# Two first projection tiles ordered by hand, the last tile's q and k and the group matrices moved, two attention groups combined on another engine

## The chip, the cores and the metric

The kernel runs on one core of a Trainium2 chip. The core has a matrix engine (TensorE, PE in the profile), a vector engine (VectorE, DVE), a scalar engine (ScalarE, ACT), a general engine (GpSimd, POOL) and SyncE (SP), which here only issues transfers. Each engine works through its own instructions in order and waits for others by semaphores. SP, ACT and POOL each have a DMA queue. The metric is the device time of one launch in microseconds (us), less is better.

## What is computed

One layer of a diffusion backbone for 256 prompt tokens and 2048 latent tokens of width 1024. Cut to what matters:

```python
h = rms_norm(x, norm1_g) * (1 + sc1) + sh1
q, k, v, f = project(h, w_in, q_norm_g, k_norm_g)      # q, k normalised by head half; 512 columns each
q, k = rope(q), rope(k)                                # latent tokens only
s = einsum('bqhmd,bkhmd->bhmqk', q, k) * scale         # 4 heads, 2 halves m
p = softmax(s)
attn = (p[:, :, 0] - lam * p[:, :, 1]) @ v             # latent tokens: 512 cached and 2048 own keys
four = fft2(f, axes=(positions, channels)).real @ w_four[group]
x = x + g1 * concat(rms_norm(attn, subln_g), four) @ w_out
x = x + g2 * relu(h2 @ w1) ** 2 @ w2
```

`lam` comes from four lambda vectors, `sc`, `sh` and `g` from conditioning vectors.

## The kernel before

Products are done at single precision in three passes, high by high, low by high and high by low parts (`mm3`, L86 to L88), so each operand is split into a rounded half and a rest: a cast on ACT, a subtraction on DVE. The stages follow one another: conditioning and head (to 41 us), first projection with the weights' splitting (to 66), the other projection tiles (to 501), Fourier mixing (to 595), attention (to 1355), output projection, MLP.

**Projection.** There are 18 tiles of 128 tokens, 0 and 1 of the prompt, 2 to 17 latent. `proj(i, g)` multiplies tile i by one of four column groups (0 q, 1 k, 2 v, 3 Fourier) into a PSUM bank, `PJ`, of which there are four, 24 products each. Ahead of it stand `norm` (L178 to L186: square on ACT, power on POOL, scale on DVE), `transposed` (transposes on PE, L195; copies with the modulation on ACT, `hTa`, L198; `hh` and `hl`, L229 and L230). Behind it `squares` (L245 to L250), `qk_post` (L259 to L293: `qn`, the rope or gain table `tb`, `qo`, `qt`), `v_post` (copy `vo`, L345, stores and split) and `f_post` (`fo`, L364). Tile 0 is special: the weights `w_in` come in halves and are split in the same loop over eight k steps (`wh` on ACT, L480, `wl` on DVE, L481), and the tile's own modulated transpose is made by `h_mod` (L457, L459), one column block on ACT and the next on DVE in turn, all into one tile `hTa0`. `setup_gains` (L109) fetches q and k gains and the four lambda vectors (`lq`) by six transfers of ACT's queue and works them out. A loop for tiles 1 to 16 follows; its order is left to the framework's scheduler, as is the head's.

**Written order.** From the last tile (17) on, the code stands in `tc.manual_schedule()`: each compute engine takes its instructions as written. There the Fourier operands start: f is folded with its reversed rows (`ds` and `rv` loads by SP; `e2048(t)` on DVE makes the difference `e`, split into `E_h` and `E_l`, and the sum in `rv`, whose row 0 is replaced by `mid`, L596); `O` are the split sums. Cosine matrices (`c2048`, `com`/`co`) and sine matrices (`s2048`, `som`/`so`), 512 KB for each of four row blocks, in the order 3, 2, 1, 0, come on POOL's queue (`dft`, L553). `E` against `c2048` gives `pabE` (48 products), `O` against `s2048` gives `pabo`. The group matrices `pabw` (L758, L759: eight small products of `wf` = w_four with `c128`, `s128`) are split into `cwh` and `cwl` (L763 to L766) and multiply every result (`py`). `evac` (L642 to L646) takes a bank out as high and low part (`abhE`, `ablE`). `head_T2` transposes the last tile's q and k (`qkT17`), which go to DRAM (`kd`, `qd`) for attention. `etmp` are two loads of the prompt's f.

**Attention.** For each of four heads, eight groups of 256 queries; a group has four units (two query blocks j, two halves m). A unit is five score blocks of 512 keys (`fill`, L875, into five PSUM banks), five row maxima on DVE (L880), five exponentials on ACT (L899). After both halves of a j, `combine` (L901 to L921) forms P0 - factor * P1 on POOL in four operations, scaled in place (L920) and added (L921), and in the very last group on DVE by five operations (L911). Then come transposes of P (`pts`, L930), their parts (`ahs` on ACT, `als` on DVE) and value products (`mul`). The order is by due times: a unit every T = 5.2, the transposes of a group from AVS = 6 units after its first.

Of the kernel before, what the change touches and what calls it, by code (L numbers as in the profile page):

```python
# [18 lines left out]
P = 128  # L19
D = 1024  # L20
KD = D // P
# [19 lines left out]
def body(tc, a, out):  # L41
    nc = tc.nc
    ctx = ExitStack()
    with ctx:
# [64 lines left out]
        def setup_gains(pool):  # L109
            for t, n, s in ((qg, "q_norm_g", 0.125), (kg, "k_norm_g", 1.0)):  # L110
                nc.scalar.dma_start(t[:, 0:64], a[n].partition_broadcast(P).rearrange("p o d -> p (o d)"))
# [5 lines left out]
            lq = pool.tile([P, 4, 64], F32, tag="t2", name="lq", bufs=6)  # L117
            for i, n in enumerate(("lambda_q1", "lambda_q2", "lambda_k1", "lambda_k2")):
                nc.scalar.dma_start(lq[:, i, :], a[n].partition_broadcast(P).rearrange("p o d -> p (o d)"))
# [84 lines left out]
        with ExitStack() as c1:  # L204
# [54 lines left out]
            def qk_post(i, ms=(0, 1), dst=None):  # L259
                s = i < 2  # L260
                if ms[0] == 0:
                    rope_load(i)
# [77 lines left out]
            def v_post(i):  # L340
                s = 1 if i < 2 else 0
                n = i if s else i - 2
                ps = PJ.pop((i, 2))
                o = t2(f"vo{i}")
                nc.scalar.copy(o, ps)  # L345
                nc.sync.dma_start(out[3][n * P:n * P + P] if s else vs[n * P:n * P + P], o)
                v_split(s, n if s else 4 + n, o, f"v{i}")
# [51 lines left out]
            with tc.manual_schedule():  # L399
# [30 lines left out]
                with tc.tile_pool(name="p0h", bufs=6, reuse_waits="tile") as halves:  # L430
# [10 lines left out]
                    for s in range(2):  # L441
                        for j in range(4):
                            nc.tensor.matmul(pm[:, 12 + j, s:s + 1], acc[s][:, j * P:(j + 1) * P], ones, start=True, stop=True)
                    for gi in range(3):
                        r = t2(f"mr{gi}")
                        (nc.vector.tensor_copy if gi == 1 else nc.scalar.copy)(r[0:2, :], pr[gi][0:2, :])
                        for j in range(4):
                            nc.tensor.transpose(pm[:, gi * 4 + j, :], r[0:2, j * P:(j + 1) * P], ident[0:2, 0:2])
                    nc.vector.tensor_add(modc[:, 0:16, :], pm, cols[:, 32:48].unsqueeze(2).to_broadcast([P, 16, 2]))
                    mk_scale(scale1, 8, 80)  # L450
                    hT = p1.tile([P, KD, P], F32, tag="hT", name="hTa0", bufs=1)
                    HH.update({i: tuple(p1.tile([P, KD, P], F32R, tag=f"h{x}", name=f"h{x}{i}") for x in "hl") for i in range(2)})

                    def h_mod(pt, k, eng):
                        sc, sh = scale1[:, k, 1:2], modc[:, k, 1:2]
                        if eng is nc.vector:
                            nc.vector.tensor_scalar(hT[:, k, :], pt[:, k % 4, :], sc, sh, op0=ALU.mult, op1=ALU.add)  # L457
                        else:
                            nc.scalar.activation(hT[:, k, :], pt[:, k % 4, :], AF.Identity, bias=sh, scale=sc)  # L459

                    def h_low(i, c):
# [1176 lines left out]
```

## Time and profile before

| | |
|---|---|
| three runs | 3042.86, 3044.54 (median), 3053.85 us |
| profiled execution: time, span | 3056.93 us, 3054.9 us |
| mean granted TensorE clock | 0.985 |
| busy: PE, DVE, ACT, POOL | 2948.1, 2019.7, 1574.5, 1054.5 us |

The profile is that of one execution. An engine's busy time is the sum of its instructions, the rest of the span it is idle. A timeline lists instructions with the idle time ahead of each and what released it; a view by stretches gives busy times and the granted clock of a part of the span. A product of 128x512 starts 0.23 us after the one before at full clock.

### The profile page before, as it was taken

The numbers are of one execution on the slowest core, as the hardware profiler recorded it, in microseconds if no ns is written. First come the engines' busy times: TensorE is split into PE (matmuls) and PEld (weight loads), VectorE is DVE, ScalarE is ACT, GpSimd is POOL, SyncE is SP. The second block draws the span as 40 slices with busy tenths as digits, with TensorE's granted clock in tenths as the row PEclk, the third lists the DMA queues.
The fourth block names the chain that finished last, engine by engine and source line by source line (L and its number), as shares of the span: only waits on it lengthen the run. The fifth ranks groups of instructions, "written<-read, shape, count | busy, mean of one in ns | idle before, by whom it ended". The sixth has DMA issues, their size and how long they took to land.

```text
span 3054.9 us, 43872 instructions
## 1 busy us (share of the span) xinstructions
PE 2948.1 (97%) x15417; PEld 2546.2 (83%) x15417; DVE 2019.7 (66%) x3370; ACT 1574.5 (52%) x3534; POOL 1054.5 (35%) x843
## 2 busy tenths in 40 slices
PE   7999998989999999989989999999999999999998
PEld 4888886768888888878879999999998887888887
DVE  6566775578888888874457667667665355454554
ACT  4233322578888888863345555555555322232221
POOL 0111112088898899852233334334332000000000
PEclk8999999999999999999999999999999999999999
DMA  7677878422121201126755546456456377555553
GB/s 275 166 198 190 222 195 261 165 76 82 34 108 42 104 31 57 69 70 205 226 167 168 168 162 213 163 166 212 163 168 224 134 248 247 172 204 168 197 206 104
DMA packets 398670, 490.87 MB, mean 161 GB/s; under 512 B 27555, under 2 KB 308208, under 8 KB 395378
## 3 DMA queue, kind: packets, MB, share of 16 engines
q1 hardware_dynamic: 390352, 473.44, 48.0%
q10 hardware_dynamic: 5506, 8.07, 0.8%
q0 software_dynamic: 2592, 6.55, 0.6%
q8 instruction: 122, 2.00, 0.3%
q14 instruction: 98, 0.80, 0.1%
HBM read 318.87 MB, written 171.18 MB: 160 GB/s over the span
## 4 chain that ended last, share of the span: by engine, by line
PE 81%; ACT 8%; DMA 4%; DVE 4%; issue 2%; POOL 1%; SPq 0%; ACTq 0%; POOLq 0%; DVEq 0%
PE ps L88 7%; PE ps L86 7%; PE ps L87 7%; PE Ss L875 7%; PE pj L86 4%; PE pj L87 4%; PE pj L88 4%; PE pts L930 3%; ACT P1s L899 3%; PE pC L1351 2%; PE pC L1350 2%; PE pC L1352 2%; PE pA L1350 2%; PE pA L1352 2%; PE pA L1351 2%; PE po L88 2%
## 5 line engine op out<-in xcount | busy, mean ns | idle before, releaser
L880 DVE TENSOR_REDUCE mxs<-Ss 128x1 f32<-128x512 f32 x640 | 419.5, 687 | 91.5 <-PE Ss L875 82.7
L921 POOL TENSOR_TENSOR P0s<-P0s,P1s 128x1024 f32<-128x1024 f32 x126 | 372.8, 2959 | 10.5
L1283 DVE TENSOR_TENSOR sl<-sr,sh 128x768 fp32r<-128x768 f32 x168 | 161.7, 964 | 279.0 <-ACT sh L1282 275.2
L1282 ACT CAST sh<-sr 128x768 fp32r<-128x768 f32 x168 | 139.7, 834 | 342.0 <-PE ps L87 335.7
L899 ACT ACTIVATE P1s<-Ss,mxs 128x512 f32<-128x512 f32 x320 | 217.1, 693 | 65.7 <-DVE mxs L883 65.7
L86 PE MATMUL pj<-wh,hh 128*128 128x512 f32 x576 | 232.4, 404 | 7.0 <-ACT vo L345 7.0
L86 PE MATMUL ps<-thT,sh 128*128 128x512 f32 x585 | 231.0, 395 | 4.8 <-ACT sh L1282 4.8
L88 PE MATMUL ps<-thT,sl 128*128 128x512 f32 x585 | 230.8, 395 | 0.5 <-DVE sl L1283 0.5
L87 PE MATMUL pj<-wl,hh 128*128 128x512 f32 x576 | 230.8, 401 | 0.2 <-DVE wl L481 0.2
L87 PE MATMUL ps<-tlT,sh 128*128 128x512 f32 x585 | 230.7, 394 | 0.0
L88 PE MATMUL pj<-wh,hl 128*128 128x512 f32 x576 | 229.0, 398 | 0.0
L1392 POOL TENSOR_TENSOR gs<-g,g 128x384 f32<-128x384 f32 x48 | 68.8, 1433 | 448.6 <-ACT g L1362 404.9
L899 ACT ACTIVATE P0s<-Ss,mxs 128x512 f32<-128x512 f32 x320 | 215.6, 696 | 10.1 <-DVE mxs L883 7.9
L875 PE MATMUL Ss<-KS1s,Qs 128*128 128x512 f32 x640 | 200.4, 427 | 13.9 <-ACT P0s L899 12.2
L1361 ACT ACTIVATE g<-uz 128x384 f32<-128x384 f32 x144 | 75.7, 526 | 251.0 <-DVE uz L1384 226.9
L875 PE MATMUL Ss<-KS0s,Qs 128*128 128x512 f32 x640 | 195.9, 418 | 8.2 <-ACT P1s L899 4.9
L930 PEld LDWEIGHTS pts<-ident,P0s 128*128 128x128 f32 x1280 | 158.8, 142 | 52.2 <-PE Ss L875 5.7
L930 PE MATMUL pts<-ident,P0s 128*128 128x128 f32 x1280 | 193.1, 274 | 6.3 <-DVE alp L1027 4.1
L920 POOL TENSOR_SCALAR P1s<-P1s,tots 128x1024 f32<-128x1024 f32 x126 | 169.1, 1342 | 5.7
L86 PE MATMUL ps<-ophT,sh 128*128 128x512 f32 x423 | 166.7, 394 | 2.6 <-ACT sh L1282 1.5
L941 DVE TENSOR_TENSOR als<-pts,ahs 128x512 fp32r<-128x512 f32 x256 | 163.9, 682 | 5.5 <-ACT ahs L936 5.4
L88 PE MATMUL ps<-ophT,sl 128*128 128x512 f32 x423 | 166.6, 394 | 0.8 <-DVE sl L1283 0.8
(575 smaller groups left out, 8277.1 us busy)
## 6 DMA issues: line engine op xcount, KB each, us to landing
sr<-sd SPq DMA_DIRECT2D x84, 768.0 KB, 4.8
a<-in_w SPq DMA_DIRECT2D x184, 256.0 KB, 3.5
b<-in_w SPq DMA_DIRECT2D x176, 256.0 KB, 4.6
sd<-gs SPq DMA_DIRECT2D x192, 192.0 KB, 1.8
sd<-g SPq DMA_DIRECT2D x144, 192.0 KB, 1.9
wm<-in_w_mod SPq DMA_DIRECT2D x32, 512.0 KB, 5.3
Qs<-qd SPq DMA_DIRECT2D x32, 512.0 KB, 3.4
hr<-hd SPq DMA_DIRECT2D x21, 768.0 KB, 5.5
```

Source lines behind the costliest of these rows:

```text
L86: nc.tensor.matmul(ps, lh, rh, start=first, stop=False)
L87: nc.tensor.matmul(ps, lh, rl, start=False, stop=False)
L88: nc.tensor.matmul(ps, ll, rh, start=False, stop=last)
L875: nc.tensor.matmul(S[:, :w], self.Q[:, x, m, j * P:j * P + P], self.hd.KS[m][:, b * 512:b * 512 + w], start=(x == 0), stop=(x == 1))
L880: nc.vector.tensor_reduce(self.mx[j][:, m, b:b + 1], self.S[j, m, b], axis=AX.X, op=ALU.max)
L899: nc.scalar.activation(dst, S, AF.Exp, bias=self.mx[j][:, m, 6:7], accum_out=self.sm[j][:, m, b:b + 1])
L920: nc.gpsimd.tensor_scalar(p, p, tot[:, 3:4], 0.0, op0=ALU.mult, op1=ALU.add)
L921: nc.gpsimd.tensor_add(d, d, p)
L930: nc.tensor.transpose(pt[:, c:c + P], self.p0[j][:, (kb + t) * P:(kb + t + 1) * P], ident)
L941: nc.vector.tensor_sub(t, self.pt[kb], f32(self.A[kb][0]))
L1282: nc.scalar.copy(hi, src)
L1283: nc.vector.tensor_sub(lo, src, f32(hi))
```

## The change

Four places change; the products are the same in number and operands.

- First tiles: `h_mod` does tile 0's first four blocks on ACT and the others on DVE, into two tiles; one of the modulation rows goes ahead of the conditioning products; `load_gains` is split off from `setup_gains`, on POOL's queue and earlier. Tile 2's load, tile 1's split and tile 2's norm stand inside the weight loop. Tile 0's `f_post` and `v_out` (a part of `v_post`), then tile 1's first two projections and tile 0's remaining work are written in order inside the manual schedule, tile 3's load behind them. The loop over tiles skips those for i = 1.
- Last tile: its rope table is loaded first; `c128`, `s128` and `wf` come on POOL's queue right after the cosine matrices; `qk_post` for q and k alternates with `e2048(1)` and `e2048(0)`; the row copy from `mid` is on POOL; the O splits are moved behind the E products; in the built program the loads of `etmp` stand ahead of those of rv1 and rv0 on SP's queue.
- Group matrices: `group_mats(0)` ahead of the E products, `group_mats(1)` behind; the evacuations of E are spread; `head_T2` takes q at step 0 and k at step 2.
- Attention: in the first two groups of head 0 the j = 1 combination is done on DVE in five operations, and the transposes start 5 units after the first unit instead of 6.

```diff
@@ -106,17 +106,21 @@
-def setup_gains(pool):
-    for t, n, s in ((qg, "q_norm_g", 0.125), (kg, "k_norm_g", 1.0)):
-        nc.scalar.dma_start(t[:, 0:64], a[n].partition_broadcast(P).rearrange("p o d -> p (o d)"))
+def load_gains(pool):
+    for t, n in ((qg, "q_norm_g"), (kg, "k_norm_g")):
+        nc.gpsimd.dma_start(t[:, 0:64], a[n].partition_broadcast(P).rearrange("p o d -> p (o d)"))
+    lq = pool.tile([P, 512], F32, tag="ff", name="lq", bufs=4)[:, 0:256].rearrange("p (n d) -> p n d", d=64)
+    for i, n in enumerate(("lambda_q1", "lambda_q2", "lambda_k1", "lambda_k2")):
+        nc.gpsimd.dma_start(lq[:, i, :], a[n].partition_broadcast(P).rearrange("p o d -> p (o d)"))
+    return lq
...
+def setup_gains(pool, lq):
+    for t, s in ((qg, 0.125), (kg, 1.0)):
...
-    lq = pool.tile([P, 4, 64], F32, tag="t2", name="lq", bufs=6)
-    for i, n in enumerate(("lambda_q1", "lambda_q2", "lambda_k1", "lambda_k2")):
-        nc.scalar.dma_start(lq[:, i, :], a[n].partition_broadcast(P).rearrange("p o d -> p (o d)"))
@@ -258,7 +262,7 @@
-if ms[0] == 0:
+if i not in RP:
@@ -337,13 +341,19 @@
-def v_post(i):
+def v_out(i):
...
+    return o
...
+def v_post(i):
+    s = 1 if i < 2 else 0
+    n = i if s else i - 2
+    o = v_out(i)
@@ -438,42 +448,47 @@
-for s in range(2):
-    for j in range(4):
-        nc.tensor.matmul(pm[:, 12 + j, s:s + 1], acc[s][:, j * P:(j + 1) * P], ones, start=True, stop=True)
-for gi in range(3):
...
+def mod_cols(gi):
...
+mod_cols(0)
+for s in range(2):
+    for j in range(4):
+        nc.tensor.matmul(pm[:, 12 + j, s:s + 1], acc[s][:, j * P:(j + 1) * P], ones, start=True, stop=True)
+mod_cols(2)
+mod_cols(1)
...
-hT = p1.tile([P, KD, P], F32, tag="hT", name="hTa0", bufs=1)
+lq = load_gains(p1)
...
-def h_mod(pt, k, eng):
+def h_mod(dst, pt, k, eng):
...
-        nc.vector.tensor_scalar(hT[:, k, :], pt[:, k % 4, :], sc, sh, op0=ALU.mult, op1=ALU.add)
+        nc.vector.tensor_scalar(dst, pt[:, k % 4, :], sc, sh, op0=ALU.mult, op1=ALU.add)
...
-        nc.scalar.activation(hT[:, k, :], pt[:, k % 4, :], AF.Identity, bias=sh, scale=sc)
...
-def h_low(i, c):
-    nc.vector.tensor_sub(HH[i][1][:, c, :], hT[:, c, :], f32(HH[i][0][:, c, :]))
...
+        nc.scalar.activation(dst, pt[:, k % 4, :], AF.Identity, bias=sh, scale=sc)
...
+h0 = [t2(f"hTa0_{b}").rearrange("p (k t) -> p k t", k=4) for b in range(2)]
+for k in range(4):
+    h_mod(h0[0][:, k, :], pt0[0], k, nc.scalar)
+    h_mod(h0[1][:, k, :], pt0[1], 4 + k, nc.vector)
...
-    for k in range(b * 4, b * 4 + 4):
-        h_mod(pt0[b], k, nc.vector if k % 2 else nc.scalar)
-    c = slice(b * 4, b * 4 + 4)
-    nc.vector.tensor_copy(HH[0][0][:, c, :], hT[:, c, :])
-    h_low(0, c)
+    hi, lo = (x[:, b * 4:b * 4 + 4, :] for x in HH[0])
+    nc.vector.tensor_copy(hi, h0[b])
+    nc.vector.tensor_sub(lo, h0[b], f32(hi))
...
-PJ.update({(0, g): pp.tile([P, 512], F32, tag="pj", name=f"pj0_{g}", bufs=4) for g in range(4)})
+PJ.update({(0, g): pp.tile([P, 512], F32, tag="pj", name=f"pj0_{g}", bufs=4) for g in (3, 2, 0, 1)})
...
+load(2)
@@ -481,21 +496,27 @@
-            if 2 <= k < 6:
-                for x in (2 * k - 4, 2 * k - 3):
-                    h_mod(pt1[x // 4], x, nc.scalar)
+            if 1 <= k < 5:
+                for x in (2 * k - 2, 2 * k - 1):
+                    h_mod(hT[:, x, :], pt1[x // 4], x, nc.scalar)
+            if k == 5:
+                nc.scalar.copy(HH[1][0], hT)
+                nc.vector.tensor_sub(HH[1][1], hT, f32(HH[1][0]))
+            if k == 6:
+                norm(p1, X[2], "a2")
...
-        nc.scalar.copy(HH[1][0], hT)
-        h_low(1, slice(0, KD))
-        load(2)
-        setup_gains(p1)
-po = c1.enter_context(tc.tile_pool(name="p1o", bufs=2, reuse_waits="tile"))
-squares(0, 0)
-squares(0, 1)
-qk_post(0)
-v_post(0)
-f_post(0)
+    po = c1.enter_context(tc.tile_pool(name="p1o", bufs=2, reuse_waits="tile"))
+    f_post(0)
+    vo0 = v_out(0)
+    proj(1, 0)
+    squares(0, 0)
+    squares(0, 1)
+    proj(1, 1)
+    setup_gains(p1, lq)
+    qk_post(0)
+    v_split(1, 0, vo0, "v0")
+    load(3)
@@ -505,14 +526,15 @@
-if i + 1 < N1:
+if i > 1:
...
-proj(i, 0)
+    proj(i, 0)
...
-if i + 2 < N1:
+if 1 < i < N1 - 2:
...
-proj(i, 1)
+if i > 1:
+    proj(i, 1)
@@ -529,6 +551,7 @@
+rope_load(LAST)
@@ -562,6 +585,8 @@
+c128, s128 = (fa.tile([P, P], F32, tag=x, name=x, bufs=1) for x in ("c128", "s128"))
+wf = fa.tile([P, 4, P], F32, tag="wf", name="wf", bufs=1)
@@ -577,6 +602,9 @@
+nc.gpsimd.dma_start(c128, a["c128"])
+nc.gpsimd.dma_start(s128, a["s128"])
+nc.gpsimd.dma_start(wf, a["w_four"][0].rearrange("g p c -> p g c"))
@@ -593,7 +621,7 @@
-V.tensor_copy(r[0:1, :], mid[0:1, :])
+nc.gpsimd.tensor_copy(r[0:1, :], mid[0:1, :])
@@ -603,15 +631,12 @@
-for t in (1, 0):
-    e2048(t)
+for m in range(2):
+    qk_post(LAST, (m,), qko)
+    e2048(1 - m)
...
-for t in ROWS:
-    O[t] = split(DR[t][1], f"O{t}_")
-qk_post(LAST, (0,), qko)
-qk_post(LAST, (1,), qko)
@@ -723,16 +748,10 @@
-ptq = [pp.tile([P, 512], F32, tag="y", name=f"pt{LAST}_{m}", bufs=3) for m in (1, 0)]
+ptq = [pp.tile([P, 512], F32, tag="y", name=f"pt{LAST}_{m}", bufs=3) for m in range(2)]
...
-c128 = fw.tile([P, P], F32, tag="c128", name="c128")
-s128 = fw.tile([P, P], F32, tag="s128", name="s128")
-wf = fw.tile([P, 4, P], F32, tag="wf", name="wf")
-nc.sync.dma_start(c128, a["c128"])
-nc.sync.dma_start(s128, a["s128"])
-nc.sync.dma_start(wf, a["w_four"][0].rearrange("g p c -> p g c"))
@@ -747,33 +766,50 @@
-paE = [pab(f"E{g}") for g in range(4)]
-for t in (3, 2, 1, 0):
-    for g in range(4):
-        ab_mm(paE[g], g, E[t], co[t], 512, t == 3, t == 0)
-A = [evac(paE[0], 0, 512, "E0")]
-for h in range(2):
-    pw = pab(f"w{h}")
+pws, paE = [pab("w0")], [pab(f"E{g}") for g in range(4)]
+pws.append(pab("w1"))
...
+def group_mats(h):
...
-        nc.tensor.matmul(pw[:, j * 256:j * 256 + P], c128, wf[:, 2 * h + j, :], start=True, stop=True)
-        nc.tensor.matmul(pw[:, j * 256 + P:j * 256 + 256], s128, wf[:, 2 * h + j, :], start=True, stop=True)
+        nc.tensor.matmul(pws[h][:, j * 256:j * 256 + P], c128, wf[:, 2 * h + j, :], start=True, stop=True)
+        nc.tensor.matmul(pws[h][:, j * 256 + P:j * 256 + 256], s128, wf[:, 2 * h + j, :], start=True, stop=True)
...
+def group_parts(h):
...
-    pv = pw.rearrange("p (g t c) -> p g t c", g=2, t=2)
+    pv = pws[h].rearrange("p (g t c) -> p g t c", g=2, t=2)
...
-    cw += [(r[:, j], l[:, j]) for j in range(2)]
-A += [evac(paE[g], 0, 512, f"E{g}") for g in range(1, 4)]
+    cw.extend((r[:, j], l[:, j]) for j in range(2))
...
+A = [None] * 4
...
+def e_evac(g):
+    A[g] = evac(paE[g], 0, 512, f"E{g}")
...
+group_mats(0)
+for t in (3, 2, 1, 0):
+    for g in range(4):
+        ab_mm(paE[g], g, E[t], co[t], 512, t == 3, t == 0)
+group_parts(0)
+for t in range(4):
+    O[t] = split(DR[t][1], f"O{t}_")
+group_mats(1)
+e_evac(0)
+group_parts(1)
+e_evac(1)
...
+    if g < 2:
+        e_evac(g + 2)
...
-    if g < 2:
-        parts[g] = head_T2(1 - g, ptq[g])
+    if g in (0, 2):
+        parts[1 - g // 2] = head_T2(g // 2, ptq[g // 2])
@@ -849,6 +885,8 @@
+self.vcomb = 5 if self.last else 5 if hd.h == 0 and g < 2 else 0
@@ -904,14 +942,15 @@
-if self.last and j:
-    for b in range(self.hd.nbk):
+if j and self.vcomb:
+    for b in range(self.vcomb):
...
-    return
-for x in range(2):
+    if self.vcomb == self.hd.nbk:
+        return
+for x in range(j and self.vcomb // 2, 2):
@@ -1084,8 +1123,9 @@
+avs = AVS - (h == 0 and g < 2)
...
-    w = base + (AVS + q) * T
+    w = base + (avs + q) * T
@@ -1098,7 +1138,7 @@
-w = base + (AVS + 5) * T + 1.0 * u
+w = base + (avs + 5) * T + 1.0 * u
```

## The prediction

> **What bounds the kernel now.** I read the busy times first, then the same by stretches of the span, to see where TensorE (PE), which carries the kernel, is not full.
>
> ```profile
> PE 2948.1 (97%) x15417; PEld 2546.2 (83%) x15417; DVE 2019.7 (66%) x3370; ACT 1574.5 (52%) x3534; POOL 1054.5 (35%) x843
> ```
>
> ```profile
> 45.00:72.00 27.00, 22.61 (x97) 17.78 (x95) 20.87 (x40) 20.19 (x42) 1.09 (x2) 0.94 0.81 286
> 72.00:80.00 8.00, 4.74 (x11) 3.77 (x12) 6.46 (x13) 4.21 (x10) 3.46 (x2) 0.50 0.32 105
> 80.00:120.00 40.00, 40.00 (x193) 32.91 (x193) 20.99 (x36) 10.28 (x21) 6.19 (x3) 0.99 0.60 165
> 520.00:560.00 40.00, 35.38 (x161) 28.73 (x162) 24.64 (x47) 14.83 (x28) 3.17 (x6) 0.86 0.52 141
> 612.00:650.00 38.00, 28.84 (x123) 20.46 (x122) 26.34 (x51) 26.60 (x74) 28.62 (x20) 0.85 0.16 57
> 770.00:860.00 90.00, 88.92 (x556) 75.29 (x555) 78.39 (x155) 79.58 (x228) 80.64 (x64) 1.00 0.17 60
> ```
>
> Columns: stretch, length, then busy time of PE, weight loads, DVE, ACT, POOL, then granted clock, DMA share, GB/s. Within stages (80:120, 770:860) PE has no gap. The change touches three seams where it has: the first tile's end (72:80: 4.74 of 8 us, clock 0.50), the passage into the Fourier stage (520:560, 4.6 us idle) and attention's start (612:650, 9.2 us idle at clock 0.85). It neither adds nor removes a matrix product, so time can come only from gaps and from half-clock stretches.
>
> **Part 1, the first two tiles.** These rows are the timeline around the first gap.
>
> ```profile
> 36.28 0.41 DVE L457 TENSOR_SCALAR hTa<-pta,scale,modc 128x128 f32<-128x128 f32 x1 [0.53 <-ACT hTa L459]
> 65.88 0.39 PE L87 MATMUL pj<-wl,hh 128*128 128x512 f32 x1
> 66.11 0.40 PE L88 MATMUL pj<-wh,hl 128*128 128x512 f32 x1
> 70.06 0.29 DVE L120 TENSOR_TENSOR lq<-lq 128x128 f32<-128x128 f32 x1 [2.95 <-DMA lq<-in_lambda_k]
> 70.81 2.88 ACT L198 ACTIVATE hTa<-pta,modc,scale 128x128 f32<-128x128 f32 x8
> 74.53 1.23 DVE L230 TENSOR_TENSOR hl<-hTa,hh 128x1024 fp32r<-128x1024 f32 x1
> 75.06 0.65 ACT L364 ACTIVATE fo<-pj 128x512 f32<-128x512 f32 x1
> 75.26 0.80 PE L86 MATMUL pj<-wh,hh 128*128 128x512 f32 x1 [7.00 <-ACT vo L345]
> 75.85 0.63 PE L87 MATMUL pj<-wl,hh 128*128 128x512 f32 x1
> 76.28 0.63 PE L88 MATMUL pj<-wh,hl 128*128 128x512 f32 x1
> ```
>
> Columns here and in the later timelines: start, duration, engine and line, operation and tiles, and in brackets the idle time before and its releaser.
> (a) The gap. Tile 0's products end at 66.5 and tile 1's begin at 75.26, because the same ACT and DVE queues first do tile 2's transposed copies (hTa, 2.88), the lambda row (DVE waits 2.95 us for a load) and only then empty the four product banks (fo, 75.06). Afterwards the order is written out: tile 2's eight transposes (1.1 us of PE that stays) stand inside tile 0's last k step, the gains and lambda rows are loaded early from POOL's queue, and fo is the first copy. fo stands behind hTa on ACT: transposes from 63.6, hTa to 67.7, fo to 68.3. PE's last product moves to 67.2 + 0.4 = 67.6, so it still waits some 0.7. Tile 1 starts at 68.3 where it was 75.26: **-7.0**. Bounds: -7.7 if fo never waits, -5 if hTa and fo are late by 2 us.
> (b) The half clock. After the gap products start 0.43 apart (75.85, 76.28), against 0.23 ahead of it (65.88, 66.11). The 80:120 stretch with its clock of 0.99 puts the end at about 80.8, so 13 products lose 0.2 each: **-2.6** if a wait of 0.7 doesn't lower the clock, 0 if it does.
> (c) The head. The first tile's scaling alternates ACT and DVE, each waiting 0.53 for the other (row 36.28), four times over. Split by halves, four operations of 0.41 run on each side at once, and the first product comes about **-1.5** sooner (0 if the weight loads then decide).
> (d) The price: tile 1's hl (1.23, by tile 2's row of that shape) and its hh, tile 2's square and scale move into the weight loop, which feeds PE from ACT and DVE. In 45:72 DVE is idle 6.1 us and ACT 6.8, so about 2 us on each is covered on the average, but not everywhere: bounds 0 and +2, I take **+0.6**. Six DMA issues leave ACT's queue there, and take POOL's, which is busy 1.09 us in that stretch.
> Part 1: -7.0 - 2.6 - 1.5 + 0.6 = **-10.5**, bounds -3 and -12, of which -8 to -12 is my own range.
>
> On the clock, the Trainium skill (TensorE: Matmul & The Clock Gate, What's actually happening) has an idle window of some 3.4 us, running free, behind each halving. The 7.00 us gap with the 0.43 spacing behind it agrees; by that rule 0.7 us costs nothing, the same as (b) takes.
>
> **Part 2, into the Fourier stage.** First the chain of waits (start, length, what), then timelines of PE, SP's queue, POOL and DVE, and the median landing time of the second matrix's loads.
>
> ```profile
> 499.53 17.16 DMA qd<-qkT_0l
> 516.72 3.80 DMA rp<-in_rope
> ...
> 528.75 0.43 PE pabo L86
> ```
>
> ```profile
> 514.16 0.39 PE L88 MATMUL pabE<-c,E_l 128*128 128x512 f32 x1
> 521.76 0.77 PE L758 MATMUL pabw<-wf,c 128*128 128x128 f32 x2 [7.21 <-DMA wf<-in_w_four]
> ...
> 526.67 0.80 PE L758 MATMUL pabw<-wf,c 128*128 128x128 f32 x2 [2.86 <-DVE ablE L646]
> ```
>
> ```profile
> 518.00 0.38 SPq L735 DMA_DIRECT2D wf<-in_w_four  x1
> ```
>
> ```profile
> 494.24 2.37 POOL L553 DMA_DIRECT2D c<-in_c  x4
> ...
> 499.50 2.17 POOL L553 DMA_DIRECT2D s<-in_s  x4
> ```
>
> ```profile
> 506.01 0.69 DVE L593 TENSOR_TENSOR e<-ds,rv 128x512 f32<-128x512 f32 x1 [8.22 <-DMA rv<-frev]
> ...
> 510.92 0.42 DVE L596 COPY rv<-mid 1x512 f32<-1x512 f32 x1
> ```
>
> ```profile
> s<-in_s POOLq DMA_DIRECT2D x4, 512.0 KB, 10.1
> ```
>
> Between the E products (last at 514.16) and pabo (528.75) PE waits 7.21 us for wf, which SP issued only at 518.00 behind the q stores (chain: 17.16 us), and 2.86 us for DVE, whose q and k work hung on the rope table (3.80 us more). Afterwards rope and wf are loaded early, q and k stand in DVE's idle 8.22 us, and the group products are split: the first half ahead of the E products, the second behind them. Both old waits go (-10.1), but two new ones can come.
> First, wf. It is on POOL's queue now, behind four c loads and two small ones: 494.24 + 2.37 + 3 x 0.59 = 498.4 for its issue. It may be there when PE is ready (501.6, no wait) or land as late as the s loads do, 10.1 us after the issue: 508.5, a wait of 6.9. With 2 MB ahead of it on its queue I take 506, a wait of 4.4, and all the E products and everything on PE are behind it. As after the 7.00 us gap, products then start at half clock for a while: 8 x 0.2 = 1.6. The E products end at 514.6 + 4.4 + 1.6 + 1.0 (first half of the group products) = 521.6.
> Second, the s loads. The copy of rv's row (DVE, 0.42) goes to POOL, where it waits for DVE's second-last add, and the four s loads, issued at 499.50 so far, are queued behind it. rv(1) comes 1 to 2 us after 506.01, since two loads of 256 KB are moved ahead of it on SP; then DVE does e(1) (2.1: three operations of 0.69), k's part (about 3.1: four of 0.7 and a 0.29) and two of e(0) (1.4): 507.5 + 6.6 = 514.1. With the copy and four issues (2.17) the last load is out at 516.7. It was 10.1 us on its way in a full stretch; it is alone now, so I take 7: 523.7. pabo, which reads the matrix of the first rows, loaded last, starts near 524 instead of 528.75: **-5**. Bounds: s at the full 10.1 (526.8) gives -2; no wait for wf, and s in time, gives 515.6 + 1 = 517, -11.
> The four O splits (0.69 each on DVE) are moved behind the E products; they have until pabo, 2 us or more.
>
> The Trainium skill (SBUF — State Buffer, SBUF: two separate sides) warns that loads issued from GpSimd starve while DVE holds the shared port in some of its operations. Here four issues took 2.37 us beside DVE work and 2.17 us after it, 0.05 us each. If each of the three new issues waited for a DVE operation of 0.69, this would add 2 us to wf, inside the bounds above.
>
> **Part 3, attention's start.** DVE's timeline in the fourth slot, the one operation of the new kind that the trace has (the very last group), POOL's combination that it replaces, and the first exponential of four units on ACT.
>
> ```profile
> 619.17 0.16 DVE L904 RECIPROCAL tots<-tots 128x1 f32<-128x1 f32 x1
> 619.25 1.27 DVE L880 TENSOR_REDUCE mxs<-Ss 128x1 f32<-128x512 f32 x2
> 620.70 2.02 DVE L880 TENSOR_REDUCE mxs<-Ss 128x1 f32<-128x512 f32 x3 [0.18 <-PE Ss L875]
> ```
>
> ```profile
> 1329.45 3.43 DVE L911 SCALAR_TENSOR_TENSOR P0s<-P1s,tots,P0s 128x512 f32<-128x512 f32 x5 [0.48 <-POOL tots L905]
> ```
>
> ```profile
> 620.22 1.12 POOL L920 TENSOR_SCALAR P1s<-P1s,tots 128x1024 f32<-128x1024 f32 x1
> ...
> 625.42 3.45 POOL L921 TENSOR_TENSOR P0s<-P0s,P1s 128x1536 f32<-128x1536 f32 x1
> ```
>
> ```profile
> 623.03 0.69 ACT L899 ACTIVATE P1s<-Ss,mxs 128x512 f32<-128x512 f32 x1 [0.48 <-DVE mxs L883]
> ...
> 628.42 0.69 ACT L899 ACTIVATE P0s<-Ss,mxs 128x512 f32<-128x512 f32 x1 [1.94 <-DVE mxs L883]
> ...
> 635.98 0.69 ACT L899 ACTIVATE P1s<-Ss,mxs 128x512 f32<-128x512 f32 x1 [1.48 <-DVE mxs L883]
> ...
> 642.96 0.69 ACT L899 ACTIVATE P0s<-Ss,mxs 128x512 f32<-128x512 f32 x1
> ```
>
> POOL took 620.22 to 628.87, 8.65 us, for one combination; DVE takes 3.43 plus the 0.48 wait for POOL's factor, so the first value products can start a slot sooner. What that costs: on DVE the five operations stand right behind the reciprocal, ahead of the row maxima of unit 5, which were ready. Those come 3.9 us later, the exponentials of unit 5 at 626.9 and not 623.03, and PE's next score products wait for the banks that ACT frees. The same again four units on. I take 3.9 + 3.4 = +7.3, less what comes back: the slots with value products move one ahead, so there is one slot without them later, where the trace shows what such a slot takes when nothing is late: 5.4 us (623.03 to 628.42) in the start, against 90 / 16.4 = 5.46 in the steady stretch, so near nothing, or 3.5 us (ACT's five exponentials at 0.69) at best. Between these and with some of the 9.2 us that PE idles in 612:650 filled, -2.3: **+5**. Bounds: +10 if PE also stays at half clock for longer (mean 0.85 of 38 us as it is), -1.5 if DVE's idle 11.7 us in 612:650 takes the ten operations in.
>
> **The sum.** -10.5 - 5 + 5 = **-10.5 us**. The profiled execution has a span of 3054.9 and a time of 3056.93; the shown runs have a median of 3044.54 (3042.86 to 3053.85), so that execution lay 12.4 above it. The gaps are the same in each, and I take the sum from the median: **3034**, its own range 3024 to 3042.
>
> **Rivals.** (A) All waits go and nothing new comes: -11.5, Fourier -8, attention -1.5, together -21, **3023.5**. For it: DVE's idle time at all three places; against it: the in-order queues at wf, s and unit 5. Chance 0.30.
> (B) The change hardly does what it says: wf and s only rename the wait (-2), attention costs its +7.3 and tile 0's end keeps half its gain (-6): about -1, **3043.5**. For it: stretch 520:560 has DMA at 0.52 and the loads ahead of it were 10.1 us on their way; against: the first gap has no load in it but lambda's. Chance 0.18.
> (C) Slower: the five-fold DVE operation in attention. Twice 3.9 late, value slots run at half clock as at 628.42 to 635.98 (7.56 against 5.46: +2.1 each for four), and the slot without value products costs a whole 5.46: 7.8 + 8.4 + 5.5 = +21.7, against -15.5: +6, **3051**. It decides from a price of 15.5. For it: DVE is already busy 78 of 90 us in the steady stretch, so a late row maximum is hardly caught up; against: 11.7 us idle at the start. Chance 0.11.
> My forecast keeps 0.41.
>
> About 0.5% (15.2 us) is what a measurement of this kernel can tell from no change: faster is below 3029.3, slower above 3059.8. Faster: A and an eighth of the forecast's own, 0.35. Slower: the worse part of C, 0.07. Same: 0.58. The range, 3019 to 3049, reaches from A's best to between B and C.
>
> **What would show it.** Part 1: tile 1's first product near 67, spacing 0.23 behind it; wrong if ACT's fo or a weight (wl) ends a wait over 2 us. Part 2: PE's wait for wf ahead of pabE, pabo waiting on s; wrong if the group products start at 501 to 503 or pabo before 519. Part 3: unit 5's exponentials some 8 us behind unit 4's where it was 3.9, transposes (pts) inside unit 5; wrong if the distance from the first exponential to the ninth is shorter than before. The forecast fails as a whole if one of the three seams changes by over 10 us from its term.

## The result, and the profile after

The changed kernel is slower: 3059.79 us median of 7 runs (3055.41 to 3068.42) against 3048.97 (7 runs beside them), a ratio of 1.0042 (95% interval 1.0027 to 1.0058), some 13 us by the ratio and 10.8 between the medians, where 10.5 less were forecast. Its profiled execution took 3058.45 us; that of before, 3056.93, lay 8 us above its own median (from the last transposes of attention to the end it took 6 us more than any other profile here), so the two profiles are compared seam by seam and not by their spans.

First a part of the page of after, and the stretches beside those of before, in the same columns (stretch, length, busy time of PE, weight loads, DVE, ACT, POOL, granted clock, DMA share, GB/s).

```profile
PE 2939.4 (96%) x15417; PEld 2539.2 (83%) x15417; DVE 2028.0 (66%) x3379; ACT 1574.9 (52%) x3534; POOL 1044.9 (34%) x845
```

```profile
72.00:80.00 8.00, 8.00 (x36) 6.46 (x35) 4.64 (x8) 1.20 (x2) 0.60 (x1) 1.00 0.42 122
...
480.00:520.00 40.00, 26.57 (x113) 21.72 (x112) 21.90 (x41) 8.64 (x16) 16.56 (x28) 0.86 0.89 278
520.00:560.00 40.00, 40.00 (x218) 33.57 (x218) 23.95 (x43) 18.71 (x40) 1.40 (x3) 0.96 0.50 134
585.00:612.00 27.00, 14.95 (x50) 8.65 (x48) 14.19 (x28) 12.30 (x34) 3.84 (x4) 0.87 1.00 383
...
650.00:700.00 50.00, 42.85 (x238) 35.08 (x239) 39.37 (x78) 38.78 (x111) 34.43 (x34) 0.93 0.24 88
```

The first gap is gone (72:80: PE 8.00 of 8 at clock 1.00). Three others take its place. At 480:520 PE is idle 13.4 us. Two of the stretches of before, which weren't shown there, tell the rest:

```profile
585.00:612.00 27.00, 21.97 (x122) 16.52 (x121) 15.38 (x31) 16.29 (x44) 3.88 (x4) 0.96 0.94 369
650.00:700.00 50.00, 48.62 (x305) 40.63 (x303) 41.99 (x83) 43.87 (x127) 44.98 (x40) 1.00 0.31 118
```

At 585:612 PE is busy 7.0 us less, at 650:700, where it had been nearly full, 5.8 less, with the clock down from 1.00 to 0.93. By the start times of the same instructions in the two profiles (after less before, from PE's timelines):

| at | before | after | difference |
|---|---|---|---|
| first product of tile 0 | 40.91 | 39.88 | -1.0 |
| first product of tile 1 | 75.26 | 66.90 | -8.4 |
| last projection product | 501.35 | 490.50 | -10.9 |
| first pabo product | 528.40 | 519.66 | -8.7 |
| last Fourier product (py) | 594.32 | 585.71 | -8.6 |
| first score product | 595.65 | 594.10 | -1.6 |
| last transposes of attention | 1347.54 | 1356.18 | +8.6 |

So the first tiles gave 10.9 us, the passage into the Fourier stage took 2.2 of it back, the start of attention 7.0 more, and attention 10.2. The +8.6 lies within the interval of the runs.

**First tiles.** The timeline of after (start, duration, engine and line, operation, idle time before and its releaser):

```profile
62.62 1.03 PE L199 MATMUL pta<-ident,x 128*128 128x128 f32 x8
63.25 2.90 ACT L202 ACTIVATE hTa<-pta,modc,scale 128x128 f32<-128x128 f32 x8 [1.57 <-PE pta L199]
...
66.25 0.60 ACT L374 ACTIVATE fo<-pj 128x512 f32<-128x512 f32 x1
...
66.90 0.50 PE L86 MATMUL pj<-wh,hh 128*128 128x512 f32 x1 [0.69 <-ACT fo L374]
...
67.24 0.40 PE L87 MATMUL pj<-wl,hh 128*128 128x512 f32 x1
67.47 0.39 PE L88 MATMUL pj<-wh,hl 128*128 128x512 f32 x1
```

Tile 2's transposes are inside tile 0's last k step, fo is the first copy behind hTa, PE waits 0.69 for it, and the products behind are 0.23 apart: no half clock.

**Into the Fourier stage.** PE, then POOL:

```profile
497.30 0.77 PE L774 MATMUL pabw<-wf,c 128*128 128x128 f32 x2 [6.41 <-DMA wf<-in_w_four]
...
498.71 0.63 PE L775 MATMUL pabw<-wf,s 128*128 128x128 f32 x2
499.00 0.77 PE L86 MATMUL pabE<-c,E_h 128*128 128x512 f32 x1
...
519.66 0.77 PE L86 MATMUL pabo<-s,O_h 128*128 128x512 f32 x1 [7.03 <-DMA s<-in_s]
```

```profile
483.08 2.20 POOL L576 DMA_DIRECT2D c<-in_c  x4
...
486.31 0.82 POOL L607 DMA_DIRECT2D wf<-in_w_four  x1
489.40 1.66 POOL L254 TENSOR_TENSOR qrs<-qss,mhalf 128x8 f32<-128x8 f32 x1 [2.27 <-DVE qss L253]
506.59 1.06 POOL L624 COPY rv<-mid 1x512 f32<-1x512 f32 x1 [15.53 <-DVE rv L622]
507.61 2.21 POOL L576 DMA_DIRECT2D s<-in_s  x4
```

wf took 11.0 us from its issue to PE, with the four c loads ahead of it, and the whole E work stood behind it. POOL then waited 15.53 us with the row copy, and the four s loads behind that copy landed 9.8 us after the last was issued (507.61 + 2.21 to 519.66). This chain, and not wf, sets pabo: the E products and the second half of the group products were done by 512.6, and PE then waited for s.

The chain begins with rv1, whose sum the row copy waits behind on DVE. SP's queue, before and after, and DVE after:

```profile
495.91 1.34 SPq L567 DMA_DIRECT2D rv<-frev  x2
```

```profile
489.29 3.49 SPq L766 DMA_DIRECT2D etmp<-fp  x2
...
494.23 0.80 SPq L592 DMA_DIRECT2D rv<-frev  x2
```

```profile
500.13 0.69 DVE L621 TENSOR_TENSOR e<-ds,rv 128x512 f32<-128x512 f32 x1 [7.83 <-DMA rv<-frev]
```

Behind the two etmp loads, rv1 is issued only 1.7 us sooner than before, though the projection ends 10.9 sooner. It reaches DVE 9.6 us behind the last projection product, where it was 4.7 before (506.01 and 501.35).

**Keys.** SP's queue and PE at attention's start:

```profile
566.41 0.33 SPq L892 DMA_DIRECT2D Qs<-qd  x1
584.59 0.33 SPq L863 DMA_DIRECT2D KS0s<-kd  x1
```

```profile
594.10 4.30 PE L913 MATMUL Ss<-KS0s,Qs 128*128 128x512 f32 x10 [8.12 <-DMA KS0s<-kd]
```

The key load of head 0 is issued just behind the last pabl product (584.28, 0.28 long); PE, done with the Fourier stage at 585.7, waits 8.12 us for it. Before, the same load went out 10 us ahead of the last pabl product, and PE waited only for a PSUM bank:

```profile
583.10 0.33 SPq L827 DMA_DIRECT2D KS0s<-kd  x1
```

```profile
595.65 2.60 PE L875 MATMUL Ss<-KS0s,Qs 128*128 128x512 f32 x10 [1.05 <-ACT ys L634]
```

**Attention.** DVE's combinations, and ACT's first exponentials of units 4, 5, 8 and 9:

```profile
617.73 3.41 DVE L949 SCALAR_TENSOR_TENSOR P0s<-P1s,tots,P0s 128x512 f32<-128x512 f32 x5 [1.50 <-POOL tots L943]
621.06 3.07 DVE L918 TENSOR_REDUCE mxs<-Ss 128x1 f32<-128x512 f32 x5
...
645.08 3.43 DVE L949 SCALAR_TENSOR_TENSOR P0s<-P1s,tots,P0s 128x512 f32<-128x512 f32 x5 [0.48 <-POOL tots L943]
```

```profile
615.99 0.69 ACT L937 ACTIVATE P0s<-Ss,mxs 128x512 f32<-128x512 f32 x1 [1.18 <-DVE mxs L921]
...
624.43 0.69 ACT L937 ACTIVATE P1s<-Ss,mxs 128x512 f32<-128x512 f32 x1 [4.99 <-DVE mxs L921]
...
643.17 0.69 ACT L937 ACTIVATE P0s<-Ss,mxs 128x512 f32<-128x512 f32 x1 [0.97 <-DVE mxs L921]
...
651.79 0.69 ACT L937 ACTIVATE P1s<-Ss,mxs 128x512 f32<-128x512 f32 x1 [3.08 <-DVE mxs L921]
```

Five row maxima that could run at once stand behind each combination; ACT idles 4.99 and 3.08 us for them, and units 4 and 8 take 8.45 and 8.62 us where before they took 3.93 and 5.44.

### The profile page after: what moved, and what is told of

Same layout as the page of the kernel before. It is cut to its first block, busy times and chain, and to the rows that moved or that the text cites. A ratio compares the mean times of both kernels' runs of the same rounds, so it can differ in the third digit from the quotient of the medians.

```text
span 3056.5 us, 43869 instructions
## 1 busy us (share of the span) xinstructions
PE 2939.4 (96%) x15417; PEld 2539.2 (83%) x15417; DVE 2028.0 (66%) x3379; ACT 1574.9 (52%) x3534; POOL 1044.9 (34%) x845
## 4 chain that ended last, share of the span: by engine, by line
PE 80%; ACT 8%; DVE 4%; DMA 3%; issue 2%; POOL 1%; SPq 0%; ACTq 0%; POOLq 0%; DVEq 0%
PE Ss L913 7%; PE ps L88 7%; PE ps L86 7%; PE ps L87 7%; PE pj L87 4%; PE pj L86 4%; PE pj L88 4%; PE pts L969 3%; ACT P1s L937 3%; PE pA L1390 2%; PE pC L1391 2%; PE pC L1390 2%; PE pA L1391 2%; PE pC L1392 2%; PE pA L1392 2%
## 5 line engine op out<-in xcount | busy, mean ns | idle before, releaser
L960 POOL TENSOR_TENSOR P0s<-P0s,P1s 128x1024 f32<-128x1024 f32 x122 | 359.6, 2947 | 10.2
```

Source lines behind the costliest of these rows:

```text
L960: nc.gpsimd.tensor_add(d, d, p)
```

## The experiments

Ratios are to the kernel before, with 95% intervals. Times of single instructions are from each run's own profile.

### Each part alone

`front_only` is the kernel before with the first place of the change only.

> Only the first two tiles are changed (part 1), the rest is as before. Theory S (each seam has its own price and they add): tile 17's last projection product comes 10.9 us sooner than before (490.5 against 501.4), and the first pabo product too, at about 517.5 against 528.4; time about 10.9 us under before, ratio 0.9965. Rival T (the passage into the Fourier stage is set by transfers that don't start sooner by as much): pabo at 523 to 528, and at most half of the 10.9 us is left in the time, ratio 0.998 to 1.000.

Measured: 0.9976 (0.9963 to 0.9989), 7.3 us less. The last projection product came at 490.47, 10.9 sooner, but pabo at 523.44, 5.0 sooner. PE, and SP's queue:

```profile
519.99 0.77 PE L780 MATMUL pabw<-wf,c 128*128 128x128 f32 x2 [16.05 <-DMA wf<-in_w_four]
```

```profile
515.57 0.38 SPq L757 DMA_DIRECT2D wf<-in_w_four  x1
```

With the order of before, wf is issued 2.4 us sooner though PE is there 10.9 sooner, so PE's wait grew from 7.21 to 16.05 us. Rival T holds for the passage (pabo in its 523 to 528): 5 us are left there, 6.0 at the last Fourier product, and the time lies between the two theories.

`part2_only` is the kernel before with the second and third place only.

> Only the last tile, the Fourier passage and its tiles are changed (part 2); first tiles and attention are as before. Theory S: from the last projection product to the first pabo product it takes about as long as in the changed kernel, 29 us (before 27), or a little less since the loads had 11 us more; the last key load is held by the last Fourier product, so the first score product comes 8 to 9 us behind it and not 1.3; together 4 to 9 us slower than before, ratio 1.0015 to 1.003. Rival (part 2 pays where the projection ends later): pabo 5 us or more sooner than before at 523 or less, and the time within 2 us of before.

Measured: 1.0034 (1.0019 to 1.0048), a little over what theory S gave. From the last projection product (502.66) to pabo (531.30) 28.6 us, where 27.1 were before; then the keys:

```profile
606.27 2.05 PE L889 MATMUL Ss<-KS0s,Qs 128*128 128x512 f32 x4 [8.16 <-DMA KS0s<-kd]
```

The 8.16 us are there with no change ahead of the passage or in attention: the wait for keys belongs to this part.

`attn_only` is the kernel before with the attention part only.

> Only attention is changed (part 3: DVE combination in two groups, transposes one unit sooner there). Theory S: units 4 to 5 and 8 to 9 are 8 us apart or more, the distance from the first exponential to the last grows by 7 us and the time by 7 to 9 us, ratio 1.0025 to 1.003. Rival D (attention's loss in the changed kernel came from its late K loads and the half clock behind them): with K loads as before the distance stays within 2 us, ratio 1.000.

Measured: 1.0035 (1.0020 to 1.0049), 10.7 us. From the first exponential to the last 730.9 us, 8.7 more than before (722.2); units 4 and 8 took 7.44 and 8.62. Rival D fell: the price is there with the keys in time. The three ratios multiply to 1.0045; together they gave 1.0042. By the ratios the parts add, within their intervals.

### The changed kernel without its attention part

`no_attn` takes the lines of the attention part back to those of before:

```diff
-self.vcomb = 5 if self.last else 5 if hd.h == 0 and g < 2 else 0
...
-if j and self.vcomb:
+if self.last and j:
...
-avs = AVS - (h == 0 and g < 2)
...
-    w = base + (avs + q) * T
+    w = base + (AVS + q) * T
```

> The changed kernel without part 3. Theory S: 7 to 9 us under the changed kernel, so about 3 to 5 us over before, ratio 1.001 to 1.002; the first score product still at about 594. Rival D: about as the changed kernel, ratio 1.004, with units at the start as far apart as there.

Measured: 0.9983 (0.9968 to 0.9997), faster than before, and further from the changed kernel than expected: its last transposes came 13.5 us sooner. Its first score product was at 593.53, as late as in the changed kernel. The first exponentials of units 8 and 9:

```profile
636.53 0.69 ACT L935 ACTIVATE P0s<-Ss,mxs 128x512 f32<-128x512 f32 x1
...
641.97 0.69 ACT L935 ACTIVATE P1s<-Ss,mxs 128x512 f32<-128x512 f32 x1 [1.01 <-DVE mxs L919]
```

Unit 8 takes 5.44 again. Attention, from the first score product to the last transposes, is 749 to 755 us long, 752 on the mean, in the nine kernels here with the attention of before, and 762 in the three with the attention part (after, `attn_only`, `k_region` below): 10 us.

### The two halves of the attention part

`vcomb_only` keeps DVE's combination and puts the transposes back to 6 units; `avs_only` does the reverse.

```diff
-avs = AVS - (h == 0 and g < 2)
+avs = AVS
```

```diff
-self.vcomb = 5 if self.last else 5 if hd.h == 0 and g < 2 else 0
+self.vcomb = 5 if self.last else 0
```

> The changed kernel with the transposes of the two groups back at 6 units (only the DVE combination is left of part 3). In the changed kernel the distance from unit 4's first exponential to unit 16's is 81.7 us, without part 3 it is 69.3. Theory V (the five DVE operations ahead of the row maxima are the price): units 4 and 8 still take 7.4 and 8.6 us, the distance stays at 76 us or more. Rival W (the price is that transposes and their copies meet the combination in the same units): the distance is 71 to 74.

> The changed kernel with POOL's combination in all groups but the last, and the transposes still one unit sooner in two groups. Theory V: PE waits for POOL's combination in units 5 and 9, 1 to 4 us each, units 4 and 8 are back at 3.9 and 5.4, and the distance from unit 4 to unit 16 is 71 to 75 us. Rival W: the distance stays at 76 or more.

Each of the two ran once. The length of units (us between first exponentials), by unit, each from one profile:

| unit | no_attn | after | vcomb_only | avs_only |
|---|---|---|---|---|
| 4 | 3.94 | 8.45 | 7.44 | 3.94 |
| 5 | 5.19 | 7.90 | 5.86 | 7.25 |
| 6 and 7 | 12.19 | 10.83 | 14.87 | 12.45 |
| 8 | 5.44 | 8.62 | 8.60 | 5.57 |
| 9 | 5.45 | 6.92 | 5.40 | 5.40 |
| 13 | 6.56 | 6.23 | 6.55 | 6.22 |
| 15 | 7.29 | 8.91 | 7.30 | 7.36 |
| 4 to 16 | 69.2 | 81.7 | 79.2 | 72.0 |

The rows behind unit 8 of `vcomb_only`:

```profile
645.46 0.69 ACT L937 ACTIVATE P0s<-Ss,mxs 128x512 f32<-128x512 f32 x1
...
654.06 0.69 ACT L937 ACTIVATE P1s<-Ss,mxs 128x512 f32<-128x512 f32 x1 [4.18 <-DVE mxs L921]
```

Theory V holds for the distances: the combination alone costs 10.0 of the 12.5 us, 6.7 of them in units 4 and 8, where it stands ahead of the row maxima. Another 2.7 are in units 6 and 7, but these vary by as much among kernels with POOL's combination (14.5 us in before, 12.2 in `no_attn`), so they aren't shown to be a price of it. The earlier transposes alone cost 2.8, 2.1 of them in unit 5; the profile has no wait of PE for POOL's combination in units 5 and 9, where theory V had one. They give next to nothing back: unit 13, which then has no transposes, is 0.3 us shorter.

### The keys' place in memory

In the built program the byte ranges in each partition are, for the change:

```
KS0s (keys of head 0)      186336 to 196576
s256_1l (last split, read by the last pabl product)  191456 to 193504
e256_0, o256_0 (read by pabf)  187360 to 191456, 183264 to 187360
```

Before, the same keys lay over e256_0 and earlier tiles, and s256_1l at 178144, outside. Two things moved it: c128, s128 and wf (3 KB) are now in the pool that lies on that side, and the O splits and k's transposes take the ring's buffers in another order. The order decides: the buffer that s256_1l now takes, once E3_l's, lay at 194528 before, inside the keys' range too. Which of the two moves changes the order was not tried. Before, the key load went out (583.10) right behind the last product that reads e256_0 (582.79), and now right behind the last that reads s256_1l (584.28), which stands some 10 us further on in the order of work. `k_region` allocates the value tile first, so that the keys lie over tiles that are done sooner; no instruction changes its place.

```diff
 self.KS = []
+self.V = ak.tile([P, self.nkt, 2, P], F32R, tag=f"V_{self.s}", name=f"V{self.nm}")
...
-self.V = ak.tile([P, self.nkt, 2, P], F32R, tag=f"V_{s}", name=f"V{self.nm}")
```

> The changed kernel with the value tile allocated ahead of the key tiles, so that the keys of head 0 no longer lie where the last Fourier operand (s256_1l) lay; the order of work is the same. Theory S (memory reuse holds the key load until the last Fourier product): the key load is issued near 566, right behind the query load, the first score product starts near 587 and not 594, and the time falls by about 7 us against the changed kernel (ratio about 1.002 to before). Rival (the key load was late for transfers or its stores): issue and first score product stay at 584 and 594.

Measured: 1.0006 (0.9991 to 1.0020). SP's queue, then PE:

```profile
567.33 0.38 SPq L864 DMA_DIRECT2D KS0s<-kd  x1
```

```profile
587.54 2.59 PE L913 MATMUL Ss<-KS0s,Qs 128*128 128x512 f32 x10 [1.06 <-ACT ys L659]
```

The load goes out 17.3 us sooner, right behind the query load, and PE's wait of 8.12 us becomes 1.06 for a PSUM bank, as before. The last transposes come 6.0 us sooner. The rival (stores or transfers) fell. The value load, now over s256_1l, goes out at 585.13 in its place, and PE doesn't wait for it.

### Together, and the passage

`best0` has both: no attention part, value tile first.

> The changed kernel without part 3 and with the value tile allocated ahead of the key tiles. Theory S (the prices add): first score product near 587, attention as long as before, the whole 5.2 + 6.5 us under the time before, ratio about 0.996. Rival: with attention starting sooner the transfers of queries and values end the wait, and the two gains don't add: ratio 0.998, as without part 3 alone.

Measured: 0.9977 (0.9964 to 0.9990), no better than `no_attn` beyond the intervals. The first score product came at 587.44, but at unit 16 only 1.3 us were left of the 6.1: units 0 to 3 took 19.6 us (16.4 in `no_attn`), 6 and 7 took 14.9 (12.2). The gains don't add, as the rival had it, but its reason isn't borne out: up to unit 8 PE waits 0.5 us for queries (1.4 in `no_attn`) and never for values. What differs is the granted clock (third number from the end). Units 6 and 7 in `best0`, `no_attn` and the next kernel, `pool_order`, which starts attention sooner still:

```profile
620.29:635.22 14.93, 12.23 (x46) 9.69 (x47) 8.62 (x17) 9.52 (x25) 9.71 (x7) 0.66 0.10 36
```

```profile
624.35:636.53 12.18, 9.35 (x47) 7.56 (x48) 8.28 (x17) 9.53 (x25) 10.96 (x7) 0.86 0.12 44
```

```profile
616.16:627.04 10.88, 8.05 (x47) 6.46 (x48) 8.28 (x17) 9.42 (x26) 9.79 (x7) 1.00 0.14 49
```

So 2.7 us of the loss come with a longer half clock in these two units, and an earlier start doesn't bring it of itself. Units 0 to 3 take 18.8 to 20.7 us in all nine kernels whose keys are there in time and 16.4 to 17.4 in the five whose keys are late; part of that is half clock too (0.83 in `best0`, 1.00 in `no_attn`), the rest was not found.

`pool_order` is `best0` with this:

```diff
+nc.gpsimd.dma_start(c128, a["c128"])
+nc.gpsimd.dma_start(s128, a["s128"])
+nc.gpsimd.dma_start(wf, a["w_four"][0].rearrange("g p c -> p g c"))
 for t in (3, 2):
...
-nc.gpsimd.dma_start(c128, a["c128"])
-nc.gpsimd.dma_start(s128, a["s128"])
-nc.gpsimd.dma_start(wf, a["w_four"][0].rearrange("g p c -> p g c"))
...
-nc.gpsimd.tensor_copy(r[0:1, :], mid[0:1, :])
+V.tensor_copy(r[0:1, :], mid[0:1, :])
```

> The kernel before it in this list (no part 3, value tile first) with the two small matrices and wf ahead of the cosine matrices on POOL's queue, and the copy of rv's row back on DVE, so that no sine load waits for it. Theory Q (both waits at the passage come from the place in POOL's queue): the group products start at 490 to 491 and not 497, the waits for wf and for the s loads are gone, pabo starts at 512 to 515 and not 519, and the time falls by 4 to 7 us, ratio about 0.994. Rival T (the passage is set by transfers, 90% of the DMA engines are busy): another load is late in their place, rv1 or rv0 or the s loads, and pabo stays at 517 to 520.

Measured: 0.9960 (0.9943 to 0.9977). PE, then DVE:

```profile
490.95 0.38 PE L774 MATMUL pabw<-wf,c 128*128 128x128 f32 x2
...
506.00 0.80 PE L86 MATMUL pabE<-c,E_h 128*128 128x512 f32 x1 [7.12 <-ACT E_h L626]
```

```profile
504.60 0.69 DVE L621 TENSOR_TENSOR e<-ds,rv 128x512 f32<-128x512 f32 x1 [12.07 <-DMA rv<-frev]
```

Both waits of theory Q are gone (wf is there at 490.95, pabo doesn't wait for s), and, as rival T had it, another load is late: rv1, issued at 490.00, reaches DVE at 504.60, now that the s loads run beside it. pabo at 516.96, between the two theories; the ratio is below those of `best0` and `no_attn` all the same, though the intervals overlap. In this build the etmp loads also stand behind rv1 on SP's queue (506.04).

`s_gate` adds a tiny POOL copy from rv1's sum ahead of the s loads; `rv_ahead` instead puts the loads of rv1 and rv0 ahead of mid and the key stores; `rv_ahead_gate` has both.

```diff
+gate = p1.tile([P, 512], F32, tag="ff", name="gate", bufs=4)
+nc.gpsimd.tensor_copy(gate[0:1, 0:128], DR[1][1][0:1, 0:128])
 for t in ROWS:
     so[t] = dft(som[t], "s2048", t)
```

```diff
+for t in (1, 0):
+    d_load(t, 1)
 mid = p1.tile([P, 512], F32, tag="ff", name="mid", bufs=4)
 ...
 k_store(0, LAST + 1, parts[0])
-for t in (1, 0):
-    d_load(t, 1)
```

> The kernel with the changed order on POOL's queue, and a tiny POOL copy that reads the sum row of rv1 ahead of the four sine loads, so that they are issued only when rv1 is there. Theory T (rv1 was late because 2 MB of sine loads share the DMA engines with it): rv1's wait on DVE falls from 12.1 us to 4 to 8, the wait of PE ahead of the third block of E products from 7.5 to 3 or less, and pabo starts at 510 to 514 (it was 516.96), ratio 0.993 to 0.995. Rival Q (rv1 is late for its own place on SP's queue): its wait stays over 10 us, the sine loads come later still, and pabo starts at 518 or later.

> The kernel with the changed order on POOL's queue, with the loads of rv1 and rv0 issued ahead of the stores of keys and of the middle row on SP's queue; the framework puts the two etmp loads ahead of them there. Theory T: with the sine loads still beside them rv1 lands 2 to 5 us sooner, pabo at 513 to 516. Rival Q (place on SP's queue decides): rv1 lands 8 us or more sooner and the wait ahead of the third block is gone, pabo at 508 to 511.

> Both of the last two: rv1 and rv0 ahead on SP's queue, and the sine loads held until rv1 is there. Theory T: rv1 lands at 494 to 498, the E products run through by 505, and pabo waits for the sine loads, 508 to 512. Rival Q: as the kernel with rv ahead and no gate, or later because the sine loads start later.

Measured: 0.9951 (0.9936 to 0.9966), 0.9936 (0.9911 to 0.9960) and 0.9932 (0.9909 to 0.9955). DVE's wait for rv1 in `s_gate`, then in `rv_ahead`, and pabo in `rv_ahead`:

```profile
497.04 0.69 DVE L621 TENSOR_TENSOR e<-ds,rv 128x512 f32<-128x512 f32 x1 [5.39 <-DMA rv<-frev]
```

```profile
495.75 0.69 DVE L621 TENSOR_TENSOR e<-ds,rv 128x512 f32<-128x512 f32 x1 [3.40 <-DMA rv<-frev]
```

```profile
508.10 0.50 PE L86 MATMUL pabo<-s,O_h 128*128 128x512 f32 x1 [1.29 <-DVE ablE L671]
```

Both causes show: with the s loads away from beside rv1 its wait falls from 12.07 to 5.39 (theory T, pabo at 511.19), with an earlier place on SP's queue to 3.40 (rival Q, pabo in its 508 to 511). In these profiles rv1 was also issued 2.1 and 2.4 us sooner than in `pool_order`; from issue to use it took 9.1 and 8.1 us, where it was 14.6. Both together give 3.51 and pabo at 508.97, no more than the place alone, as rival Q had it; pabo waits 1.30 for DVE there, and not for the s loads as theory T had it. From the last projection product to pabo it is 17.6 us now, where it was 27.1 before and 29.2 after the change. The last two kernels, about 20 us under the time before, are the best; they and `s_gate` don't differ beyond their intervals.

## Why the prediction was wrong

It forecast 3034 with a range of 3019 to 3049; it came out at 3059.79, on the other side of no change. Of the 25.8 us between, 4.4 lie in the median of before that it starts from: 3044.54 in the three runs shown, 3048.97 in seven. Most of the rest shows in the seams, which by the table gave +8.6 for a forecast of -10.5: the first tiles -10.9 for -10.5, the passage +2.2 for -5, a wait for keys +7.0 with no term, attention +10.2 for +5. Part by part:

- **Part 1 was right** in each step: tile 1 at 66.90 (68.3 less 1.5 is 66.8), a wait of 0.69 for fo (0.7), 0.23 between products behind it, -10.9 at the end of the projections (-10.5). No price in the weight loop showed in the sum. The head gave 1.0 in this pair of profiles; over all of them its first product comes at 40.9 to 42.2 in the three kernels with the old head and 38.8 to 40.2 in the others, which fits the forecast 1.5 as well.
- **Adding part 1 to part 2 was sound here, but not of itself.** Between `part2_only` and the changed kernel, the same from the last tile to attention, the last projection product is 12.2 us apart and the first score product 12.2. With the old order `front_only` had 10.9 us ahead of the passage and 5.0 behind it: there the gain is worth only what the passage's loads also come sooner.
- **Part 2's term failed: +2.2 for -5.** Its chain was named rightly and sized too low. The prediction had rv1 at DVE 6.1 us behind the last projection product (507.5 against 501.35), the copy at 0.42 and the last s load 7 us under way because it would be "alone now". They took 9.6, 1.06 and 9.8 (10.1 in the full stretch of before): 3.5, 0.6 and 2.8 us more, together 6.9 of the 7.2 missed. So pabo was to come at 524 - 10.5 = 513.5 and came at 519.66. The biggest of the three is rv1, taken as 1 to 2 us late for the two loads ahead of it on SP's queue. wf was taken 4.4 us late, with 6.9 as a bound: 6.41, but pabo waited for s all the same. `pool_order` showed that the place in POOL's queue made both of PE's waits.
- **Part 2 had no term for memory.** Nothing in the prediction asked which tile's buffer the first key load takes over. It was the largest cost without any term: 7.0 us, told apart by `k_region`.
- **Part 3 had the right mechanism and a wrong balance.** The price of late row maxima, 3.9 + 3.4, measured 3.5 in unit 4 of `vcomb_only` and 3.2 in unit 8. The credit of 2.3 for idle PE time and for a slot without value products didn't come (0.3 in unit 13). Instead, against `no_attn`, units 5, 9 and 15 grew by 2.7, 1.5 and 1.6. Unit 5 grew by 2.1 with the earlier transposes alone. Units 5 and 9 hold PE's longest gaps at attention's start, 6.5 and 3.2 us, and the clock of 650:700 is 0.93. So +10 and not +5, at the bound of +10, which the prediction gave for a longer half clock.

Unit 15 grows only with both halves of the part, and there it is the clock (0.81 and 1.00 in these stretches of the changed kernel and `avs_only`):

```profile
688.78:697.69 8.91, 6.72 (x33) 5.62 (x34) 5.72 (x11) 5.71 (x14) 6.87 (x6) 0.81 0.09 21
```

```profile
680.47:687.83 7.36, 5.12 (x33) 4.29 (x34) 5.75 (x11) 5.60 (x15) 6.86 (x6) 1.00 0.00 0
```

PE's longest wait there is nearly the same in both, 2.37 and 2.39 us. In the traces the granted clock changes only at steps of 3.41 us. In the changed kernel the wait lies whole in one step (686.68 to 690.09, PE busy 1.04 us) and the next step has half clock; in `avs_only` it is split between two steps (busy 2.89 and 1.55) and the clock stays full.

**Rival C** foretold a loss, but by attention alone at a price of 21.7; that was 10. The range ended at 3049, between B and C: C had a chance of 0.11, and no case had part 2 losing.

## What to carry to other kernels

A gain ahead of a stage that is timed by loads has to be followed to the end of that stage before it is added to anything. Moving small tiles to another pool, or changing the order in which a ring of buffers is taken, can move the next stage's first load over a tile that lives to the last instruction: look up which buffer each first load of a stage takes over. An operation put on an in-order engine costs what waits behind it, even where that engine is idle a third of the time on the average; and a load belongs on its queue by when it is needed, ahead of bulk that is needed later.

## What the hardware showed

A 256 KB load (rv1) took 14.6 us from issue to use with 2 MB of other loads beside it (`pool_order`), 9.1 with those held back and 8.1 from an earlier place on its queue. The one-partition copy of 512 elements took 1.06 us on POOL, 0.42 on DVE. DVE's combination of five times 128x512 took 3.41 to 3.43 us at attention's start as it had in the last group. PE's idle 6.41 and 7.03 us in the changed kernel were each followed by products 0.43 apart (pairs of 128x128 at 497.86 and 498.29, pabo at 520.22 and 520.65), 0.69 us were not; the Trainium skill (TensorE: Matmul & The Clock Gate, What's actually happening), which puts an idle window of some 3.4 us behind each halving, agrees with all three. But 2.37 us were enough in unit 15 of the same kernel: PE was busy 1.04 of the 3.41 us ahead of 690.09, and score products then started 0.43 apart. So by the measurement a window need not be idle throughout.
